# Attention's value products in bursts of nine key blocks, from a ring of twelve

## The chip, the cores and the metric

The kernel runs on one core of a Trainium2 chip. The metric is device time in microseconds (us), as a median over runs. The core's engines have queues of their own and wait for one another through semaphores: TensorE (PE, with PEld for its weight loads), VectorE (DVE), ScalarE (ACT), GpSimd (POOL) and SyncE (SP, which issues most transfers).

## The reference, cut to what matters

Two layers over 2048 latent rows and 256 context rows: multi-head latent attention (16 heads), then gated linear attention. The change lies in the first. Latent queries read all 2304 keys, context queries only the 256 context keys.

```python
def attention_blocks(q, k, v):
    ...
    def one_block(qi):
        s = jnp.einsum('bqhrd,bkhd->bhrqk', qi, k, preferred_element_type=F32) * scale
        p = jax.nn.softmax(s, axis=-1).astype(v.dtype)
        return jnp.einsum('bhrqk,bkhe->bqhre', p, v)
...
def mla_mixer(...):
    oc = attention_blocks(qc, kc, vc)
    ox = attention_blocks(qx, jnp.concatenate([kc, kx], axis=1), jnp.concatenate([vc, vx], axis=1))
    def out(o, gate):
        return (o.reshape(b, n, MLA_WIDTH) * jax.nn.silu(gate)) @ w_out
```

## The kernel before, in words

**The steps.** Attention runs over 8 pairs of heads. Each pair has 5 query chunks, so there are 40 steps: chunk 0 is the 256 context queries (2 key blocks of 128), chunks 1 to 4 are 512 latent queries each (18 key blocks, `kt` 0 to 17). One item is one key block of one step, 592 in all. The order of the work is written out by hand: PE's and most of VectorE's instructions in attention stand in program order (`pe_op`), and the framework places the rest, GpSimd's among them, on in-order queues.

**One item.** First the search for row maxima of a later step is fed one move further (`stream`, L491: 4 matmuls into `pmx`, whose maxima VectorE takes at L493). Then `scores` makes 10 matmuls into `st` (L629), on half the array's rows each, and ScalarE's exponential writes the weights to a slot of `ring` (L631). The ring has 9 slots of 128 x 1024.

**The bursts.** The value products (`values`, L678, full rows and half the columns of the array, fp32 in two passes) come in bursts of six blocks: after `kt` 6 of a step for `kt` 0 to 5, and so on; the last burst of a step comes after item 0 of the next. A context step's two blocks come four items after its second one. With 8 context and 32 x 3 latent bursts, there are 104.

**The sums.** The softmax denominator is the sum of a step's weights over its blocks. VectorE sums the first three blocks of each burst in four instructions (`thirds`, L662), the first time into `acc`, later into `part`. GpSimd adds the other three blocks and `part` to `acc`, one instruction of 128 x 1024 each (`add`, L652). So a latent step has 12 VectorE sums and 11 GpSimd adds: nine blocks and two parts. Blocks that come before the first `thirds` wait in a list.

**The end of a step.** `finish` runs in the burst after a step's last one. It multiplies `acc` with ones on PE (L693, into `pmx`), ScalarE turns that into a reciprocal (L695, L696), and GpSimd scales the output (`ob`, L697). So PE's L693 waits for GpSimd's last add of the step. For chunk 4 of a pair, the next burst is the short one of the next pair's context step, five items after chunk 4's last burst began; for the other chunks it is the next step's first.

**What else GpSimd does.** It splits queries (`qs<-qf`, L48 and L53) and the keys of a later pair (`kbs<-kf`) into high and low parts. Keys go into the buffer that the running pair is reading, piece by piece as chunk 4 has read them for the last time, so five key splits fall around the last chunk of a pair.

**Other parts.** `mods` puts modulation products (L72, L86, L98) behind some bursts. `kbs0` is 8192 columns wide, of which keys use 4608. Near the end of attention `out_weights` splits the output weights into the key buffers, in pieces of 128 x 1024, on ScalarE and GpSimd.

Of the kernel before, what the change touches and what calls it, by code (L numbers as in the profile page):

```python
# [122 lines left out]
def body(ctx, tc, I, out, stop=99, dbg=None):  # L123
# [293 lines left out]

    kbs = [kvp.tile([P, 8 * D], F32R, name="kbs0"), kvp.tile([P, 4 * T], F32R, name="kbs1")]
    kb = [[kbs[b][:, s * T:s * T + T] for s in range(2)] for b in range(2)]
# [183 lines left out]
    with pool("p3", 2) as sp, pool("ps3", 2, space=PSUM) as psp:  # L603
# [5 lines left out]

        RING = 9  # L610
        ring = sp.tile([P, RING, 2, 512], F32, name="pe", bufs=1)

        def scores(si, kt, nk):
            pr, ci = steps[si]
            n = CHUNKS[ci][1]
            kh, kl = kb[pr % 2]
            qs = qss[si]
            if kt == 0:
                assert si in closed
                gt = sp.tile([P, 512], F32, name="gt")  # L620
# [9 lines left out]
            pe = ring[:, slot(si, kt)]  # L630
# [4 lines left out]
        def slot(si, kt):  # L635
            pr, ci = steps[si]
            return (75 * pr + (3 + 18 * (ci - 1) if ci else 0) + kt) % RING

# [15 lines left out]
        def thirds(si, kt):  # L654

            st_ = live[si]
            part = sp.tile([P, 2, 512], F32, name="part", bufs=1) if kt else st_["acc"]
            s0 = slot(si, kt)
            for j in range(2):
                for c in (0, 256):  # L660
                    src = ring[:, s0:s0 + 3, j, c:c + 256].rearrange("p s c -> p c s")
                    pe_op(nc.vector.tensor_reduce(part[:, j, c:c + 256], src, axis=AX.X, op=ALU.add))  # L662
            if kt:
                add(si, part)
            else:
                st_["open"] = True
                for pe in st_["wait"]:
                    add(si, pe)

        def values(si, kt, nk):  # L670
# [3 lines left out]
            if kt == 0:  # L674
                st_["po"] = psp.tile([P, 512], F32, name="po", bufs=1)
            po, pe, vt = st_["po"], ring[:, slot(si, kt)], vts[pr]
            for j in range(2):
# [42 lines left out]
        def first_y(oh, ol):  # L720

            ps = [pmp.tile([P, 512], F32, name="pmx") for _ in range(2)]
            for kt in range(KT):
                for u in range(2):
                    us = slice(u * 512, u * 512 + 512)
                    for i, (a, b) in enumerate(((oh, 0), (oh, 1), (ol, 0))):
                        nc.tensor.matmul(ps[u], a[:, kt, :], wo[kt][b][:, us], start=(kt == i == 0), stop=(kt == KT - 1 and i == 2))
            y0 = ring[:, 0]
# [14 lines left out]
        def out_weights(b, raw):  # L743

            w = kvp.tile([P, 8 * D], F32R, name=f"wo{b}", tag=f"kbs{b}")
            w2 = [w[:, 4 * D * s:4 * D * s + 4 * D].rearrange("p (k n) -> p k n", k=4) for s in range(2)]
            for kt in range(4):
                tc.keep_in_program_order(k.hi("a", w2[0][:, kt, :], raw[kt]))
                tc.keep_in_program_order(k.lo("p", w2[1][:, kt, :], raw[kt], w2[0][:, kt, :]))
                wo[4 * b + kt] = (w2[0][:, kt, :], w2[1][:, kt, :])  # L750

# [3 lines left out]
        rate = (sum(20 if ci else 2 for _, ci in steps) - fed) / (len(items) - 24)  # L755
        fed0 = fed
        pinned = True
        done, extra, nv, nb = [], mods(), 0, 0

        bursts = {i + (4 if nk == 2 else 1): i + 1 for i, (si, kt, nk) in enumerate(items) if kt % 6 == 5 or kt == nk - 1}  # L760

        def burst(i):
# [4 lines left out]
            nb += 1  # L767
            if fed < fed0 + rate * i:
                fed += 1
# [18 lines left out]
            for c in cl:  # L788
                next(c, None)
            if nb > 4 and nb % 3 == 0 and i < len(items) - 70:  # L790
                next(extra, None)

        for i, (si, kt, nk) in enumerate(items):
# [7 lines left out]
            if i % 3 == 1:  # L801
                fetch(1)
            if fed < fed0 + rate * (i + 1):
                fed += 1
# [78 lines left out]
    with pool("p4", 2) as sp, pool("ps4", 2, space=PSUM) as psp:  # L883
# [53 lines left out]
        for t in range(NT):  # L937
# [14 lines left out]
            for u in range(2 if t else 0):  # L952
                us = slice(u * 512, u * 512 + 512)
                p_ = psp.tile([P, 512], F32, name="py", bufs=3)
                k.mm3(p_, [(oh[:, kt, :], ol[:, kt, :], wo[kt][0][:, us], wo[kt][1][:, us]) for kt in range(KT)])
                ps.append(p_)
# [610 lines left out]
```

## Time and profile before

| | us |
|---|---|
| median of 3 runs | 3642.26 |
| lowest, highest | 3637.54, 3643.7 |
| profiled execution | 3641.14 |
| its span, first to last instruction | 3639.3 |
| first and last value product (L678) of attention start | 698.9, 2255.1 |

In the 1556 us of the last row all eight pairs are done. The rows are read so: the timeline merges neighbouring instructions of one kind into one line with their count, and gives in brackets the idle time ahead of it and what ended it; the waits say which engine and line waited for which; the stretches give the busy time of each engine and the clock granted to PE as a share of its full one. A matmul's end is modelled, so starts are compared with starts.

### The profile page before, as it was taken

How to read it: one execution, taken by the hardware profiler on the slowest of the kernel's cores; microseconds unless marked ns; L12 is line 12 of the kernel's file. 1: busy time of each engine (PE TensorE's matmuls, PEld its weight loads, DVE VectorE, ACT ScalarE, POOL GpSimd, SP SyncE). 2: the span in 40 equal slices, each digit the busy share in tenths (PEclk: the TensorE clock that was granted, in tenths of full speed). 3: DMA queues.
4: the chain of work that ended last, by engine and by line, in shares of the span. 5: the costliest groups of instructions: out<-in, count | busy, mean ns of one | idle time of the engine just before them, and what ended most of it. 6: DMA issues, size and time to landing. Idle time of an engine off the chain costs nothing.

```text
span 3639.3 us, 59322 instructions
## 1 busy us (share of the span) xinstructions
PE 3512.7 (97%) x24126; PEld 2657.4 (73%) x24126; DVE 2266.6 (62%) x3350; ACT 1337.6 (37%) x1951; POOL 1418.4 (39%) x873
## 2 busy tenths in 40 slices
PE   6999999999999999999999999999999999999899
PEld 5877887666666666666666665778998998998677
DVE  4333334677777777777777773563277677777753
ACT  2222121244444343444344444232244344454431
POOL 3111205366676666766676677552000001000000
PEclk9999999999999999999999999999999999999899
DMA  6111356402112111202110010777756757678432
GB/s 232 70 67 64 129 219 193 131 24 83 46 36 65 50 53 45 79 18 79 47 58 22 23 40 22 233 234 242 262 197 206 249 173 237 209 235 288 142 118 93
DMA packets 280920, 456.00 MB, mean 125 GB/s; under 512 B 23028, under 2 KB 179764, under 8 KB 268680
## 3 DMA queue, kind: packets, MB, share of 16 engines
q1 hardware_dynamic: 215760, 375.06, 31.2%
q10 hardware_dynamic: 64888, 77.16, 6.2%
q8 instruction: 189, 3.10, 0.3%
q14 instruction: 83, 0.68, 0.1%
HBM read 311.27 MB, written 140.71 MB: 124 GB/s over the span
## 4 chain that ended last, share of the span: by engine, by line
PE 78%; DMA 6%; issue 6%; DVE 5%; POOL 3%; ACT 2%; SPq 1%; ACTq 0%; POOLq 0%; DVEq 0%
PE st L629 18%; PE po L678 14%; PE pmx L491 8%; PE pj L60 5%; PE pj L62 4%; PE pj L61 4%; PE pp L985 3%; PE pp L986 3%; PE pp L987 3%; DMA wsg<-in_gla_w_in 2%; PE py L62 2%; PE py L61 2%; PE py L60 2%; PE pk L1152 1%; PE py L985 1%
## 5 line engine op out<-in xcount | busy, mean ns | idle before, releaser
L493 DVE TENSOR_REDUCE mx<-pmx 128x1 f32<-128x512 f32 (+1 forms) x1312 | 767.4, 627 | 326.6 <-PE pmx L491 316.1
L631 ACT ACTIVATE pe<-st 128x1024 f32<-128x1024 f32 (+1 forms) x592 | 600.8, 1015 | 704.1 <-PE st L629 479.1
L652 POOL TENSOR_TENSOR acc<-acc,pe 128x1024 f32<-128x1024 f32 x288 | 688.2, 2390 | 418.5 <-DVE acc L662 268.3
L629 PE MATMUL st<-qs,kbs 64*128 64x512 f32 (+3 forms) x5920 | 801.9, 390 | 1.5 <-DMA qs<-mr 1.2
L629 PEld LDWEIGHTS st<-qs,kbs 64*128 64x128 f32 (+1 forms) x5920 | 584.2, 185 | 105.1 <-ACT pe L631 4.7
L678 PE MATMUL po<-pe,vt 128*64 128x512 f32 (+1 forms) x2368 | 524.2, 591 | 0.0
L491 PE MATMUL pmx<-kbs,qs 64*128 64x512 f32 (+1 forms) x2624 | 435.4, 380 | 14.2 <-DVE mx L493 13.9
L678 PEld LDWEIGHTS po<-pe,vt 128*64 128x64 f32 x2368 | 160.6, 137 | 310.0 <-issue 306.6
L491 PEld LDWEIGHTS pmx<-kbs,qs 64*128 64x128 f32 x2624 | 271.5, 187 | 127.5 <-issue 43.3
L985 PE MATMUL pp<-w,ht 128*128 128x256 f32 x1088 | 317.3, 292 | 0.0
L986 PE MATMUL pp<-w,ht 128*128 128x256 f32 x1088 | 305.1, 280 | 0.0
L987 PE MATMUL pp<-w,ht 128*128 128x256 f32 x1088 | 304.3, 280 | 0.0
L1334 POOL TENSOR_TENSOR orr<-oss,mhalf 128x4 f32<-128x4 f32 x16 | 17.1, 1069 | 657.4 <-DVE oss L1333 657.4
L662 DVE TENSOR_REDUCE part<-pe 128x256 f32<-128x768 f32 x256 | 246.6, 1027 | 23.5 <-ACT pe L631 19.2
L985 PEld LDWEIGHTS pp<-w,ht 128*128 128x128 f32 x1088 | 204.9, 188 | 3.5
L986 PEld LDWEIGHTS pp<-w,ht 128*128 128x128 f32 x1088 | 205.1, 189 | 1.1
L987 PEld LDWEIGHTS pp<-w,ht 128*128 128x128 f32 x1088 | 204.8, 188 | 0.1
L985 PE MATMUL pp<-ht,w 128*128 128x256 f32 (+1 forms) x616 | 182.9, 297 | 10.8 <-ACT vge L1050 9.1
L119 POOL TENSOR_TENSOR rs_r<-rs_v,mhalf 128x1 f32<-128x1 f32 x52 | 29.3, 564 | 383.5 <-DVE rs_v L117 355.2
L986 PE MATMUL pp<-ht,w 128*128 128x256 f32 (+1 forms) x616 | 175.1, 284 | 0.0
L987 PE MATMUL pp<-ht,w 128*128 128x256 f32 (+1 forms) x616 | 174.3, 283 | 0.1
L1209 ACT ACTIVATE ex<-df 128x512 f32<-128x512 f32 x192 | 114.2, 632 | 145.5 <-DVE df L1206 129.1
(369 smaller groups left out, 6291.6 us busy)
## 6 DMA issues: line engine op xcount, KB each, us to landing
ht<-hh_d SPq DMA_DIRECT2D x44, 1024.0 KB
ht<-hl_d SPq DMA_DIRECT2D x44, 1024.0 KB
xt<-in_x SPq DMA_DIRECT2D x32, 512.0 KB
mod_w<-in_ada_w SPq DMA_DIRECT2D x16, 1024.0 KB
v<-gv_d SPq DMA_DIRECT2D x32, 512.0 KB
wsg<-in_gla_w_in SPq DMA_DIRECT2D x66, 192.0 KB
v_d<-vs ACTq DMA_DIRECT2D x18, 512.0 KB
vt<-v_d SPq DMA_DIRECT2D x8, 1152.0 KB
```

Source lines behind the costliest of these rows:

```text
L60: nc.tensor.matmul(ps, ah, bh, start=(i == 0), stop=False)
L61: nc.tensor.matmul(ps, ah, bl, start=False, stop=False)
L491: pe_op(nc.tensor.matmul(ps[j][:, :w], qs[js, 0, i, t * P:t * P + P], kk[js, bs], start=(i == 0), stop=(i == 1)))
L493: pe_op(nc.vector.reduce_max(mx[:, j * nq + t, b:b + 1], ps[j][:, :w], axis=AX.X))
L629: pe_op(nc.tensor.matmul(st[:, j, :n], a[js, ks], qs[js, s, r, :n], start=(i == 0), stop=(i == len(terms) - 1)))
L631: nc.scalar.activation(pe[:, :, :n], st[:, :, :n], AF.Exp, scale=SCALE)
L652: nc.gpsimd.tensor_tensor(acc, acc, part, op=ALU.add)
L662: pe_op(nc.vector.tensor_reduce(part[:, j, c:c + 256], src, axis=AX.X, op=ALU.add))
L678: pe_op(nc.tensor.matmul(po[64 * j:64 * j + 64, :n], vt[:, kt, 64 * j:64 * j + 64], pe[:, j, :n], start=(kt == 0), stop=(kt == nk - 1)))
L985: nc.tensor.matmul(ps, ah, bh, start=(i == 0), stop=False)
L986: nc.tensor.matmul(ps, ah, bl, start=False, stop=False)
L987: nc.tensor.matmul(ps, al, bh, start=False, stop=(i == n - 1))
```

## The change

The part of `kbs0` that keys leave free becomes a tile of its own, `ring3`, with three more slots: twelve slots in four groups of three, used in turn. Bursts take nine blocks, so a latent step has two; VectorE sums three blocks at `kt` 0 and at `kt` 9 (8 instructions), and GpSimd adds the other twelve blocks and one `part`. From chunk 4 of pair 6 on (`late`), ring and bursts are as before, because part of the output weights goes where `ring3` was. There are 8 + 27 x 2 + 5 x 3 = 77 bursts. The search is fed up to three moves further ahead, and several moves in one burst if it is behind; `mods` moves every second burst instead of every third; the output weights are split in pieces of 128 x 512.

```diff
-    kbs = [kvp.tile([P, 8 * D], F32R, name="kbs0"), kvp.tile([P, 4 * T], F32R, name="kbs1")]
+    kbs = [kvp.tile([P, 2 * T], F32R, name="kbs0"), kvp.tile([P, 4 * T], F32R, name="kbs1")]
+    ring3 = kvp.tile([P, 8 * D - 2 * T], F32, name="ring3")
...
-        RING = 9
-        ring = sp.tile([P, RING, 2, 512], F32, name="pe", bufs=1)
+        ring = sp.tile([P, 9, 2, 512], F32, name="pe", bufs=1)
+        threes = [ring[:, 3 * g:3 * g + 3] for g in range(3)]
+        threes.append(ring3[:, 0:3 * D].rearrange("p (s j c) -> p s j c", s=3, j=2))
+        LAST = 25 * 7 - 6
+        late = lambda si: steps[si][0] == NPAIR - 1 or steps[si] == (NPAIR - 2, len(CHUNKS) - 1)
+        bl = lambda si: 6 if late(si) else 9
+        on_v = lambda si: (0, 6, 12) if late(si) else (0, 9)
...
-            if nk == 2 or kt % 6 > 2:
+            if nk == 2 or kt - kt % 3 not in on_v(si):
                 add(si, pe)
...
+            g = 25 * pr + (1 + 6 * (ci - 1) if ci else 0) + kt // 3
+            return threes[g % 4 if g < LAST else g % 3]
...
-            w = kvp.tile([P, 8 * D], F32R, name=f"wo{b}", tag=f"kbs{b}")
...
+            w = kvp.tile([P, 8 * D if b else 2 * T], F32R, name=f"wo{b}", tag=f"kbs{b}")
+            hs = [w[:, c:c + 512] for c in range(0, (16 if b else 9) * 512, 512)]
+            if b == 0:
+                w = kvp.tile([P, 8 * D - 2 * T], F32R, name="wo2", tag="ring3")
+                hs += [w[:, c:c + 512] for c in range(0, 7 * 512, 512)]
...
+                for u in range(2):
+                    us = slice(u * 512, u * 512 + 512)
+                    h_, l_ = hs[2 * kt + u], hs[8 + 2 * kt + u]
+                    tc.keep_in_program_order(k.hi("a", h_, raw[kt][:, us]))
+                    tc.keep_in_program_order(k.lo("p", l_, raw[kt][:, us], h_))
...
-        bursts = {... if kt % 6 == 5 or kt == nk - 1}
+        bursts = {... if kt % bl(si) == bl(si) - 1 or kt == nk - 1}
...
-            if fed < fed0 + rate * i:
+            while fed < min(fed0 + EARLY * min(1, i / 100) + rate * i, 656):
...
-                if nk > 2 and kt % 6 == 0:
+                if nk > 2 and kt in on_v(si):
                     thirds(si, kt)
...
-            if nb > 4 and nb % 3 == 0 and i < len(items) - 70:
+            if nb > 4 and nb % 2 == 0 and i < len(items) - 70:
```

GpSimd's queue at the end of the last chunk of pair 2, up to the last add into that chunk's `acc` (`kbs` is a key split, `qs` a query split, `pe` and `ring` are slots of the ring). Before:

```order
L652 TENSOR_TENSOR acc<-acc,pe 128x1024 x3
L652 TENSOR_TENSOR acc<-acc,part 128x1024
L48 TENSOR_SCALAR kbs_3830<-kf 128x512
L53 TENSOR_TENSOR kbs_3830<-kf,kbs_3830 128x512
L652 TENSOR_TENSOR acc<-acc,pe 128x1024 x2
L48 TENSOR_SCALAR qs<-qf 128x1024
L53 TENSOR_TENSOR qs<-qf,qs 128x1024
L652 TENSOR_TENSOR acc<-acc,pe 128x1024
L48 TENSOR_SCALAR kbs_3830<-kf 128x512
L53 TENSOR_TENSOR kbs_3830<-kf,kbs_3830 128x512
L652 TENSOR_TENSOR acc<-acc,part 128x1024
```

Ahead of these rows stand the chunk's first three adds, an output product `ob` and a key split: from the first `thirds` on there are 11 adds and three key splits. In the changed kernel, from the fourth add on:

```order
L663 TENSOR_TENSOR acc<-acc,ring_3832 128x1024 x3
L708 TENSOR_TENSOR ob<-ob,rs 128x512
L663 TENSOR_TENSOR acc<-acc,pe 128x1024
L48 TENSOR_SCALAR kbs_3830<-kf 128x512
L53 TENSOR_TENSOR kbs_3830<-kf,kbs_3830 128x512
L663 TENSOR_TENSOR acc<-acc,pe 128x1024 x4
L48 TENSOR_SCALAR qs<-qf 128x1024
L53 TENSOR_TENSOR qs<-qf,qs 128x1024
L663 TENSOR_TENSOR acc<-acc,pe 128x1024
L48 TENSOR_SCALAR kbs_3830<-kf 128x512
L53 TENSOR_TENSOR kbs_3830<-kf,kbs_3830 128x512
L663 TENSOR_TENSOR acc<-acc,part 128x1024
```

Now three adds stand ahead, so there are 13 adds and two key splits; the third key split moved ahead of the chunk's first add. The ends of pairs 0 to 5 have this same order.

PE's queue at the first burst of the last chunk of pair 1 (`st` are scores, `po` value products, `pmx<-acc,ones` the sum of `finish`, `pmx<-ident,mc` a step of the search). Before:

```order
L629 MATMUL st<-qs,kbs_3831 128x512 x10
L678 MATMUL po<-pe,vt 64x512 x12
L693 MATMUL pmx<-acc,ones 64x512 x2
L491 MATMUL pmx<-kbs_3830,qs 128x256 x2
L491 MATMUL pmx<-kbs_3831,qs 128x256 x2
L629 MATMUL st<-qs,kbs_3831 128x512 x10
```

In the changed kernel:

```order
L636 MATMUL st<-qs,kbs_3831 128x512 x10
L492 MATMUL pmx<-kbs_3830,qs 128x512 x2
L492 MATMUL pmx<-kbs_3831,qs 128x512 x2
L689 MATMUL po<-pe,vt 64x512 x18
L704 MATMUL pmx<-acc,ones 64x512 x2
L506 MATMUL pmx<-ident,mc 8x128
L492 MATMUL pmx<-kbs_3830,qs 128x512 x2
```

The burst comes three items later, holds nine blocks instead of six, and takes the search's transposition (L506) with it, which had stood behind the chunk's second burst.

## Rows read from the trace of the kernel before

**Rows 1.** The page: busy us (share of the span) and instructions of two engines.

```profile
PE 3512.7 (97%) x24126; PEld 2657.4 (73%) x24126; DVE 2266.6 (62%) x3350; ACT 1337.6 (37%) x1951; POOL 1418.4 (39%) x873
```

**Rows 2.** Busy us of each engine in attention, 700 to 2260 us; then the granted clock.

```profile
700.00:2260.00 1560.00, 1546.39 (x11071) 973.16 (x11071) 1141.36 (x1755) 656.33 (x688) 1064.52 (x533) 1.00 0.15 47
```

**Rows 3.** Waits of PE in 700 to 2262 us: total, times, longest.

```profile
PE pmx L491 <- DVE mx L493: 8.6, 8, 1.7
PE pmx L693 <- POOL acc L652: 3.1, 1, 3.1
```

**Rows 4.** Timeline of PE around one burst of six: start, length, count.

```profile
1264.19 0.63 PE L491 MATMUL pmx<-kbs,qs 64*128 64x512 f32 x4
1264.75 5.37 PE L678 MATMUL po<-pe,vt 128*64 128x512 f32 x24
1270.05 0.27 PE L505 MATMUL pmx<-ident,mc 128*8 128x128 f32 x1
1270.25 0.73 PE L491 MATMUL pmx<-kbs,qs 64*128 64x512 f32 x4
1270.82 1.33 PE L629 MATMUL st<-qs,kbs 64*128 64x512 f32 x10
1271.98 0.62 PE L491 MATMUL pmx<-kbs,qs 64*128 64x512 f32 x4
1272.44 1.33 PE L629 MATMUL st<-qs,kbs 64*128 64x512 f32 x10
```

**Rows 5.** Timeline of PE's weight loads inside the same burst.

```profile
1265.23 0.14 PEld L678 LDWEIGHTS po<-pe,vt 128*64 128x64 f32 x2 [0.29 <-issue]
...
1269.09 0.14 PEld L678 LDWEIGHTS po<-pe,vt 128*64 128x64 f32 x2 [0.29 <-issue]
```

**Rows 6.** Timeline of POOL, chunk 4 of pair 2 from its first add.

```profile
1253.70 7.32 POOL L652 TENSOR_TENSOR acc<-acc,pe 128x1024 f32<-128x1024 f32 x3 [5.71 <-DVE acc L662]
1260.99 1.30 POOL L697 TENSOR_TENSOR ob<-ob,rs 128x512 f32<-128x512 f32 x1
1262.24 0.63 POOL L48 TENSOR_SCALAR kbs<-kf 128x512 fp32r<-128x512 f32 x1
...
1264.21 7.26 POOL L652 TENSOR_TENSOR acc<-acc,pe 128x1024 f32<-128x1024 f32 x3
...
1281.36 1.04 POOL L48 TENSOR_SCALAR qs<-qf 128x1024 fp32r<-128x1024 f32 x1
...
1284.80 2.38 POOL L652 TENSOR_TENSOR acc<-acc,pe 128x1024 f32<-128x1024 f32 x1
...
1289.56 2.40 POOL L652 TENSOR_TENSOR acc<-acc,part 128x1024 f32<-128x1024 f32 x1
```

**Rows 7.** Timeline of PE there: first burst of the chunk, and its sum.

```profile
1248.62 5.37 PE L678 MATMUL po<-pe,vt 128*64 128x512 f32 x24
...
1295.05 1.03 PE L693 MATMUL pmx<-acc,ones 128*64 128x512 f32 x4
```

**Rows 8.** Timelines of PE and POOL in chunk 4 of pair 1: first burst, last add, sum.

```profile
1047.70 2.79 PE L678 MATMUL po<-pe,vt 128*64 128x512 f32 x12
...
1088.59 2.40 POOL L652 TENSOR_TENSOR acc<-acc,part 128x1024 f32<-128x1024 f32 x1
...
1093.62 1.03 PE L693 MATMUL pmx<-acc,ones 128*64 128x512 f32 x4
```

**Rows 9.** Timeline of PE at a modulation product.

```profile
1232.88 1.92 PE L72 MATMUL pmx<-mod_w,condT 128*32 128x512 f32 x16
...
1238.52 0.72 PE L491 MATMUL pmx<-kbs,qs 64*128 64x512 f32 x3 [1.65 <-DVE mx L493]
```

**Rows 10.** Stretches after two of PE's waits: busy us by engine, then granted clock.

```profile
1240.50:1244.00 3.50, 3.50 (x26) 3.01 (x26) 1.12 (x3) 1.58 (x2) 0.00 (x0) 0.69 0.97 366
2259.80:2263.30 3.50, 3.50 (x10) 2.76 (x9) 0.55 (x2) 1.23 (x2) 3.50 (x2) 0.51 0.00 0
```

**Rows 11.** Timeline of POOL at the end of attention.

```profile
2258.77 9.40 POOL L53 TENSOR_TENSOR wo<-wso,wo 128x1024 fp32r<-128x1024 f32 x4
```

More of the change, by code (lines that the diff above doesn't have):

```diff
@@ L629, in scores, with three, weights @@
                     pe_op(nc.tensor.matmul(st[:, j, :n], a[js, ks], qs[js, s, r, :n], start=(i == 0), stop=(i == len(terms) - 1)))
-            pe = ring[:, slot(si, kt)]
+            pe = weights(si, kt)
             nc.scalar.activation(pe[:, :, :n], st[:, :, :n], AF.Exp, scale=SCALE)
-            if nk == 2 or kt % 6 > 2:
+            if nk == 2 or kt - kt % 3 not in on_v(si):
                 add(si, pe)
-        def slot(si, kt):
+        def three(si, kt):
             pr, ci = steps[si]
-            return (75 * pr + (3 + 18 * (ci - 1) if ci else 0) + kt) % RING
+            g = 25 * pr + (1 + 6 * (ci - 1) if ci else 0) + kt // 3
+            return threes[g % 4 if g < LAST else g % 3]
+        def weights(si, kt):
+            return three(si, kt)[:, kt % 3]
         def add(si, part):
@@ L657, in thirds @@
             part = sp.tile([P, 2, 512], F32, name="part", bufs=1) if kt else st_["acc"]
-            s0 = slot(si, kt)
+            t3 = three(si, kt)
             for j in range(2):
                 for c in (0, 256):
-                    src = ring[:, s0:s0 + 3, j, c:c + 256].rearrange("p s c -> p c s")
+                    src = t3[:, :, j, c:c + 256].rearrange("p s c -> p c s")
                     pe_op(nc.vector.tensor_reduce(part[:, j, c:c + 256], src, axis=AX.X, op=ALU.add))
@@ L675, in values @@
                 st_["po"] = psp.tile([P, 512], F32, name="po", bufs=1)
-            po, pe, vt = st_["po"], ring[:, slot(si, kt)], vts[pr]
+            po, pe, vt = st_["po"], weights(si, kt), vts[pr]
             for j in range(2):
@@ L726, in first_y @@
                     for i, (a, b) in enumerate(((oh, 0), (oh, 1), (ol, 0))):
-                        nc.tensor.matmul(ps[u], a[:, kt, :], wo[kt][b][:, us], start=(kt == i == 0), stop=(kt == KT - 1 and i == 2))
+                        nc.tensor.matmul(ps[u], a[:, kt, :], wo[kt][b][u], start=(kt == i == 0), stop=(kt == KT - 1 and i == 2))
             y0 = ring[:, 0]
@@ L743, in out_weights @@
         def out_weights(b, raw):
-            w = kvp.tile([P, 8 * D], F32R, name=f"wo{b}", tag=f"kbs{b}")
-            w2 = [w[:, 4 * D * s:4 * D * s + 4 * D].rearrange("p (k n) -> p k n", k=4) for s in range(2)]
-            for kt in range(4):
-                tc.keep_in_program_order(k.hi("a", w2[0][:, kt, :], raw[kt]))
-                tc.keep_in_program_order(k.lo("p", w2[1][:, kt, :], raw[kt], w2[0][:, kt, :]))
-                wo[4 * b + kt] = (w2[0][:, kt, :], w2[1][:, kt, :])
+            w = kvp.tile([P, 8 * D if b else 2 * T], F32R, name=f"wo{b}", tag=f"kbs{b}")
[3 more added lines that the diff above has]
+                hs += [w[:, c:c + 512] for c in range(0, 7 * 512, 512)]
+            for kt in range(4):
+                wo[4 * b + kt] = (hs[2 * kt:2 * kt + 2], hs[8 + 2 * kt:10 + 2 * kt])
+                for u in range(2):
[3 more added lines that the diff above has]
+                    tc.keep_in_program_order(k.lo("p", l_, raw[kt][:, us], h_))
         items = [(si, kt, (CTX if ci == 0 else T) // P) for si, (pr, ci) in enumerate(steps) for kt in range((CTX if ci == 0 else T) // P)]
@@ L756, in body @@
         fed0 = fed
+        EARLY = 3
         pinned = True
         done, extra, nv, nb = [], mods(), 0, 0
-        bursts = {i + (4 if nk == 2 else 1): i + 1 for i, (si, kt, nk) in enumerate(items) if kt % 6 == 5 or kt == nk - 1}
+        bursts = {i + (4 if nk == 2 else 1): i + 1 for i, (si, kt, nk) in enumerate(items) if kt % bl(si) == bl(si) - 1 or kt == nk - 1}
         def burst(i):
@@ L802, in body @@
                 fetch(1)
[L803 removed]
+            if fed < fed0 + EARLY * min(1, i / 100) + rate * (i + 1):
                 fed += 1
@@ L954, in body @@
                 p_ = psp.tile([P, 512], F32, name="py", bufs=3)
-                k.mm3(p_, [(oh[:, kt, :], ol[:, kt, :], wo[kt][0][:, us], wo[kt][1][:, us]) for kt in range(KT)])
+                k.mm3(p_, [(oh[:, kt, :], ol[:, kt, :], wo[kt][0][u], wo[kt][1][u]) for kt in range(KT)])
                 ps.append(p_)
```

## The prediction, made before the changed kernel was run

> **What bounds the kernel now.** I read the page first, then the stretch of attention, then the waits of PE in it, and last the timelines of PE and GpSimd at the two places that the change touches: a burst, and the end of a pair. The page shows PE busy for 97% of the span and GpSimd for 39% [rows 1]. In attention PE is busy for 1546 of 1560 us, GpSimd for 1065 and VectorE for 1141 [rows 2], so PE bounds this stage. It waits little: 8.6 us in 8 places for VectorE's maxima, and 3.1 us once, at the very end, for GpSimd's last add [rows 3]. There are thus two ways in which this change can move the time: fewer PE cycles, or new waits on PE.
>
> The reader should also see a near miss. At the end of pair 2, GpSimd's last add ends at 1289.56 + 2.40 = 1291.96, and PE's sum of it starts at 1295.05 [rows 6, 7]: a slack of 3.1 us. At the end of pair 1 it is 1093.62 - 1090.99 = 2.6 us [rows 8]. GpSimd is busy for two thirds of the stage, but right there it is nearly late.
>
> **Fewer bursts: a gain.** A burst changes how PE's array is used (half the rows for scores, half the columns for values). From the search to values it takes 1264.75 - 1264.19 = 0.56 us, from the search to scores 0.46: 0.10 more [rows 4]. The first pair of value matmuls lasts 1265.23 - 1264.75 = 0.48 us, a pair further on (1269.09 - 1265.23) / 9 = 0.43: 0.05 more. The last pair starts at 1269.52 and what follows at 1270.05: 0.10 more. The search behind the burst takes 0.57 instead of 0.46: 0.11 more [rows 4, 5]. That is 0.36 us for a burst on the path. With 104 - 77 = 27 fewer: 9.7 us gained. The bounds are 5.4 (entry and exit alone) and 9.7; I take 9.7, since all four pieces stand in the rows.
>
> The Trainium skill says in "TensorEngine Tiling (Array Packing)", Key Properties, that a change of tiling mode drains the engine, and in "TensorE: Matmul & The Clock Gate", Step-by-step: what each phase is for, that a drain is about 128 cycles. At the full clock that would be an estimate of 0.05 us each way and of 2.9 us for 27 bursts, and the sum below would end 6.8 us higher. The rows show over three times as much, and they decide.
>
> **Later and more adds on GpSimd: the loss.** At the end of a pair the sum of `finish` comes five items after the start of chunk 4's last burst, not a whole burst later as elsewhere. I compare two paths from the same point, the start of that chunk's first burst.
>
> GpSimd's path in the changed kernel: in pair 2 the first add starts 1253.70 - 1248.62 = 5.1 us after the burst, when VectorE has its three blocks. Behind it stand, without a gap, 13 adds at 2.43 us (7.32 and 7.26 for three: 31.6), one `ob` at 1.25, two key splits at 1.97 (3.9) and one query split at 1284.80 - 1281.36 = 3.44 [rows 6, 7]. The end is at 5.1 + 31.6 + 1.25 + 3.9 + 3.4 = 45.3 us. The weights that the adds read are there in time. The chunk before has the same chain without key splits, 41.4 us, and a chunk takes about 1556 / 32 = 48.6 us with its share of context steps, so GpSimd has some 7 us for the first three key splits and is free when the burst comes.
>
> PE's path: in pair 1, without a modulation on the way, it is 1093.62 - 1047.70 = 45.9 us [rows 8]. The new first burst comes three items later (3 x 1.62 = 4.9, from 1.16 + 0.46 of [rows 4]), and one burst boundary falls away (0.4). Both hold 18 blocks of values, the context's two and the same sums. That leaves 40.6 us, so PE waits for 45.3 - 40.6 = 4.7 us. The order shows this queue at the ends of pairs 0 to 5; pair 6 keeps bursts of six there. At the ends of pairs 0, 2 and 4, one modulation product lies on PE's path in the new order: 1.9 us, and a wait behind it of 1.65 less the usual 0.2 [rows 9]. There PE waits for 4.7 - 3.3 = 1.4 us. Waits: 3 x 4.7 + 3 x 1.4 = 18.3 us. Bounds: 9 (PE 1.7 us later than that throughout) and 30 (2 us sooner).
>
> After such a wait PE's clock falls. After the wait of 3.1 us in [rows 3], the granted clock is 0.51 over 3.5 us; behind the wait of 1.65 us it is 0.69 over 3.5 [rows 10]. The first costs 1.7 us of work at the full clock. I take 1.7 for each long wait and half of that for each short one: 5.1 + 2.6 = 7.7 us, with bounds of 5.1 (the long ones alone) and 15 (twice as long).
>
> The Trainium skill speaks against moving sums to GpSimd: "GPSIMD Engine Reference", Elementwise side-by-side cycle accounting and Engine selection, wants an elementwise add on VectorE and gives 4.5 us for an add of twice this size. By an estimate of 2.25 us for one, the chain would end 2.3 us sooner, the waits would be 7.2 us and the sum 11 us lower. The rows have 2.43 from start to start and decide.
>
> **What else moves.** The four VectorE instructions less per step (27 x 4) free an engine for which PE waits 8 times in all [rows 3], and the one looked at stands behind a modulation [rows 9], of which there are as many as before. I take 0; the bound is a gain of those 8.6 us. The search does the same number of moves, a few items earlier, and in the new order its results are ready eight items ahead of their use instead of five: 0. The key and query splits end 2 to 3 us later in their chunk; the first search that reads such a query stands some five items behind the pair's sum, about 8 us: 0. The ring is no tighter: a slot is written again twelve items later instead of nine, and by the chain above GpSimd's adds have left it by then. Halving the pieces of the output weights puts eight instructions in the place of four at the end, where they hold up the last output: four take 9.40 us [rows 11]; eight of half the size, at 1.3 as the lower key split in [rows 6] has (1.97 less 0.63), 10.4. A cost of 0.9 us; the same halving earlier lies beside PE's scores.
>
> **The sum.** -9.7 + 18.3 + 7.7 + 0.9 = +17.2 us on the profiled execution's 3641.1, so 3658.3. The median of the runs is 1.1 us above that execution: 3659.4. I forecast 3659 us, 0.5% slower. About 0.2%, or 7.3 us, is what a measurement here can tell from no change.
>
> **The rivals.**
> - GpSimd is not late, and only the gain is left: 3642.3 - 9.7 + 0.9 = 3633.5, faster. It needs the chain of 45.3 us to end 4.7 us sooner, which is the price of the two added adds (4.9), or PE to come as much later. For it speaks that GpSimd idles for a third of the stage. Against it: that idle time lies ahead of the chain, where it waits for VectorE's three blocks (5.7 us ahead of the first add [rows 6]), and inside the chain hardly any is left to close. Chance 8%.
> - PE comes later than I count, so the waits shrink to about 9 us and the clock falls at half the places: 3642.3 - 9.7 + 9 + 3.9 + 0.9 = 3646.4, no change that can be told. Its own waits behind the longer bursts would do that. Chance 18%.
> - The waits are as long as the upper bounds, and the clock stays low twice as long: 3642.3 - 9.7 + 30 + 15 + 0.9 = 3678.5. A key split that must wait for its transfer inside the chain would do that. Chance 9%.
> - The change doesn't do what it says: the 0.36 us are no cost of a burst but of what comes with it, such as the sums and transpositions, whose number stays. Then there is no gain, and the waits are left: 3669, inside the forecast's range. Chance 5%.
>
> **How the numbers follow.** The forecast has 60%, with a range of its own from 3648 to 3670. The range for 8 in 10 leaves out the first rival and most of the third: 3642 to 3676. Faster by over 0.2%: the first rival, 8%. Within 0.2%: the second and a little of the forecast's lower end, 19%. Slower: 73%.
>
> **What the profile after would show.** Right: PE's waits have a row of L704 (the sum, L693 before) for GpSimd's add with six more places, long ones at the ends of pairs 1, 3 and 5, each with a dip of the clock behind it; and entries and exits of bursts as long as before, only 27 fewer. Wrong: no such waits (then the first rival), or GpSimd's last add in those chunks ending less than 43 us after the chunk's first burst, or more than 47.

## The result, and the profile after

| | before | changed |
|---|---|---|
| median of 4 runs each, us | 3642.98 | 3693.80 |
| lowest, highest | 3637.54, 3643.83 | 3689.76, 3694.28 |
| ratio, 95% interval | | 1.0135 [1.0123, 1.0148] |
| span of the profiled execution | 3639.3 | 3691.7 |
| attention, first to last value product | 698.9 to 2255.1 (1556.3) | 698.2 to 2308.4 (1610.3) |

The changed kernel is 1.35% slower (51 us by the medians), where 17 us were forecast. The sign was right, the time lies outside the range. All of the loss lies in attention: +54.0 us there, and what follows the last value product takes 1384 us before and 1383 after.

The page of the changed kernel, the row that answers [rows 1]:

```profile
PE 3525.7 (96%) x24126; PEld 2693.1 (73%) x24126; DVE 2167.9 (59%) x3242; ACT 1338.6 (36%) x1959; POOL 1547.9 (42%) x935
```

VectorE has 108 instructions less and GpSimd 62 more, as planned. Now attention by engine, then granted clock, DMA share and GB/s (answers [rows 2]):

```profile
700.00:2310.00 1610.00, 1559.22 (x11060) 1007.63 (x11056) 1042.76 (x1646) 657.13 (x695) 1191.28 (x590) 0.98 0.15 46
```

PE was busy for 1546 of 1560 us before; now it idles for 51 of 1610, and the mean clock has gone from 1.00 to 0.98. What PE waits for in that stretch (total, times, longest; answers [rows 3]):

```profile
PE pmx L704 <- POOL acc L663: 14.4, 4, 5.3
PE st L636 <- DMA qs<-mr: 14.0, 2, 8.5
PE pmx L492 <- DVE mx L494: 13.1, 10, 2.2
PE pmx L492 <- ACT mod_g L100: 6.5, 2, 3.4
PE pmx L492 <- DVE mr L510: 1.3, 5, 0.3
```

Of these the kernel before had only the maxima (8.6) and one short wait for the transfer of the maxima row:

```profile
PE st L629 <- DMA qs<-mr: 1.2, 1, 1.2
```

So three kinds of wait are new: for GpSimd's sum (forecast), for the transfer that puts the row of maxima into the queries (`qs<-mr`), and for ScalarE's copy of a modulation gate (`mod_g`). With 0.2 us more on either side, waits rose from 10.0 to 49.5 us: +39.5, of which 14.4 are the sum's, 12.8 the transfer's, 6.5 the gate copies', and the rest the maxima's and their row's. The trace's clock records add up to 6.8 us at the lower of the clock's two levels (half speed) in attention before, 58.0 after. Part of that lies inside the waits: PE was busy in 44.9 of the 58.0 us, and in all of the 6.8 before. 38.1 us more of work at half speed cost some 19 us. 39.5 + 19 = 58.5 us lost, against 54 measured: 4 to 5 us are left for the gain.

**The wait that was forecast.** PE and then GpSimd at the end of pair 1 (answers [rows 8]):

```profile
1072.63 7.95 PE L689 MATMUL po<-pe,vt 128*64 128x512 f32 x36
...
1112.18 1.08 PE L689 MATMUL po<-pe,vt 128*64 128x256 f32 x8
1118.62 1.98 PE L704 MATMUL pmx<-acc,ones 128*64 128x512 f32 x4 [5.35 <-POOL acc L663]
```

```profile
1078.01 14.70 POOL L663 TENSOR_TENSOR acc<-acc,pe 128x1024 f32<-128x1024 f32 x6 [4.40 <-DVE acc L673]
...
1114.30 0.62 POOL L48 TENSOR_SCALAR kbs<-kf 128x512 fp32r<-128x512 f32 x1 [0.51 <-DMA kf<-k_d]
1115.00 1.26 POOL L53 TENSOR_TENSOR kbs<-kf,kbs 128x512 fp32r<-128x512 f32 x1
1116.22 2.34 POOL L663 TENSOR_TENSOR acc<-acc,part 128x1024 f32<-128x1024 f32 x1
```

GpSimd's last add ends 1116.22 + 2.34 - 1072.63 = 45.9 us after the chunk's first burst (forecast: 45.3). PE is done with its own work 1112.18 + 1.08 - 1072.63 = 40.6 us after it (forecast: 40.6).

**The wait that was not.** The end of pair 4, on PE, ScalarE's queue, SP's queue and GpSimd:

```profile
1727.55 0.79 PE L636 MATMUL st<-qs,kbs 33*128 33x512 f32 x1 [5.55 <-DMA qs<-mr]
```

```profile
1719.78 6.68 ACTq L512 DMA_DIRECT2D qs<-mr  x2
```

```profile
1710.61 1.81 SPq L453 DMA_DIRECT2D qf<-qr_d  x4
1723.35 0.34 SPq L436 DMA_DIRECT2D kf<-k_d  x1
1727.93 0.34 SPq L450 DMA_DIRECT2D qf<-qn_d  x1
```

```profile
1720.97 2.36 POOL L53 TENSOR_TENSOR qs<-qf,qs 128x1024 fp32r<-128x1024 f32 x1
1723.28 2.34 POOL L663 TENSOR_TENSOR acc<-acc,pe 128x1024 f32<-128x1024 f32 x1
1725.93 0.62 POOL L48 TENSOR_SCALAR kbs<-kf 128x512 fp32r<-128x512 f32 x1 [0.31 <-DMA kf<-k_d]
...
1727.86 2.37 POOL L663 TENSOR_TENSOR acc<-acc,part 128x1024 f32<-128x1024 f32 x1
```

Read from the last fence up: GpSimd's query split ends at 1723.3 and frees a buffer; SP can then issue the key load (1723.35), and its data are there at 1725.9. Only then does ScalarE's queue issue the second of the two small transfers: the two take 6.68 us to issue, until 1726.46. PE starts again at 1727.55. The transfer of the maxima has nothing to do with that key load by its data. What ties them is a completion semaphore: the program gives every transfer one of a few, which the transfer raises when it has landed, and the next transfer with the same one waits for that before it is issued. In the program's instructions the key load on SP and the second of ScalarE's two transfers share `DMAHW6`, one right after the other:

```
L436 DMA kf<-k_d 128x512 [waits DMAHW6_49,Pool_49]
L512 DMA qs<-mr 1x4x128 [waits DMAHW5_49,DMAHW0_49,DVE_49]
L512 DMA qs<-mr 1x4x128 [waits DMAHW6_49]
```

The end of pair 5 is the same, with 9.59 us on ScalarE's queue and 8.49 us on PE. At these two ends the late sum cannot be seen: GpSimd's last add ends at 1730.2, before PE, now itself held up by 5.55 us, comes to its sum.

**The gate copy.** The end of pair 0, on PE, ScalarE and SP's queue:

```profile
907.97 1.22 PE L492 MATMUL pmx<-kbs,qs 64*128 64x512 f32 x4 [3.10 <-ACT mod_g L100]
```

```profile
907.33 0.59 ACT L100 COPY mod_g<-pmx 128x512 f32<-128x512 f32 x1 [7.14 <-DMA gbc_d<-mod_g]
```

```profile
896.93 2.53 SPq L628 DMA_DIRECT2D gt<-gate_d  x1
900.17 0.33 SPq L450 DMA_DIRECT2D qf<-qn_d  x1
900.55 1.81 SPq L453 DMA_DIRECT2D qf<-qr_d  x4
902.41 0.43 SPq L628 DMA_DIRECT2D gt<-gate_d  x1
903.15 0.34 SPq L101 DMA_DIRECT2D gbc_d<-mod_g  x1
```

One buffer serves both gate copies of a modulation block. The first copy's store stands on SP's queue behind the loads of the next pair and leaves at 903.15; the second copy waits 7.14 us for it. PE's search waits for that copy, which reads the `pmx` buffer that the search needs next. Modulation now goes on in every second burst instead of every third, and this put a gate right behind the sum at the end of pair 0. The other wait, of 3.40 us at 1058 us, lies inside pair 1: there the first store stands behind a key load that SP issued at 1053.73, when GpSimd's query split had ended.

**The clock.** Stretches behind four of the waits (answers [rows 10]; the granted clock is the third number from the end):

```profile
896.00:900.00 4.00, 3.69 (x7) 1.38 (x8) 0.00 (x0) 1.63 (x3) 2.00 (x3) 0.64 0.63 178
...
1115.00:1122.00 7.00, 3.38 (x12) 1.48 (x14) 0.22 (x1) 1.23 (x2) 5.38 (x4) 0.54 0.41 115
...
1726.00:1733.00 7.00, 5.45 (x26) 4.26 (x28) 2.49 (x4) 2.65 (x3) 5.20 (x5) 0.54 0.29 78
1931.00:1942.00 11.00, 5.00 (x26) 3.97 (x28) 2.04 (x4) 2.65 (x3) 8.78 (x6) 0.53 0.24 64
```

With a wait of 2.1 us the clock was at its lower level for 3.4 us, with 5.4 and 5.6 us for 6.8, with 8.5 us for 10.2; with the gate copies' 3.1 and 3.4 us it was 6.8. In the long waits it fell before PE had started again, which is why the second stretch has PE idle and the clock low at once. The forecast had 3.5 us for each long wait.

**The bursts.** One of nine blocks, PE and its weight loads (answers [rows 4, 5]):

```profile
1301.43 7.95 PE L689 MATMUL po<-pe,vt 128*64 128x512 f32 x36
1309.31 0.73 PE L492 MATMUL pmx<-kbs,qs 64*128 64x512 f32 x4
1309.88 0.75 PE L636 MATMUL st<-qs,kbs 64*128 64x256 f32 x10
```

```profile
1301.92 0.14 PEld L689 LDWEIGHTS po<-pe,vt 128*64 128x64 f32 x2 [0.29 <-issue]
...
1308.35 0.14 PEld L689 LDWEIGHTS po<-pe,vt 128*64 128x64 f32 x2 [0.28 <-issue]
```

The first pair takes 0.49 us, a pair further on 0.43, the search behind it 0.57: these pieces of an entry and an exit cost what they cost before.

### The profile page after: what moved, and what is told of

Same layout as the page of the kernel before. It is cut to its first block, busy times and chain, and to the rows that moved or that the text cites. A ratio compares the mean times of both kernels' runs of the same rounds, so it can differ in the third digit from the quotient of the medians.

```text
span 3691.7 us, 59328 instructions
## 1 busy us (share of the span) xinstructions
PE 3525.7 (96%) x24126; PEld 2693.1 (73%) x24126; DVE 2167.9 (59%) x3242; ACT 1338.6 (36%) x1959; POOL 1547.9 (42%) x935
## 4 chain that ended last, share of the span: by engine, by line
PE 70%; DMA 8%; POOL 8%; issue 6%; DVE 5%; ACT 2%; SPq 1%; ACTq 0%; POOLq 0%; DVEq 0%
PE st L636 16%; PE po L689 11%; PE pmx L492 7%; PE pj L60 4%; PE pj L61 4%; PE pj L62 4%; POOL acc L663 4%; PE pp L1004 3%; PE pp L1006 3%; PE pp L1005 3%; DMA wsg<-in_gla_w_in 2%; PE py L1004 1%; PE py L62 1%; PE py L61 1%; PE py L60 1%
## 5 line engine op out<-in xcount | busy, mean ns | idle before, releaser
L636 PE MATMUL st<-qs,kbs 64*128 64x512 f32 (+2 forms) x5920 | 839.5, 394 | 14.3 <-DMA qs<-mr 14.0
L636 PEld LDWEIGHTS st<-qs,kbs 64*128 64x128 f32 (+1 forms) x5920 | 628.7, 188 | 110.3 <-DMA qs<-mr 14.7
L638 ACT ACTIVATE pe<-st 128x1024 f32<-128x1024 f32 (+1 forms) x467 | 473.3, 1014 | 507.8 <-PE st L636 401.5
L492 PE MATMUL pmx<-kbs,qs 64*128 64x512 f32 (+1 forms) x2624 | 475.8, 383 | 25.9 <-DVE mx L494 18.0
L689 PE MATMUL po<-pe,vt 128*64 128x512 f32 (+1 forms) x1868 | 413.3, 589 | 0.0
L492 PEld LDWEIGHTS pmx<-kbs,qs 64*128 64x128 f32 x2624 | 309.6, 190 | 123.6 <-issue 39.9
L689 PEld LDWEIGHTS po<-pe,vt 128*64 128x64 f32 x1868 | 128.6, 137 | 247.8 <-issue 243.8
L1353 POOL TENSOR_TENSOR orr<-oss,mhalf 128x4 f32<-128x4 f32 x16 | 17.1, 1069 | 657.7 <-DVE oss L1352 657.7
L663 POOL TENSOR_TENSOR acc<-acc,ring 128x1024 f32<-128x1024 f32 x81 | 194.6, 2403 | 79.6 <-DVE acc L673 75.0
L638 ACT ACTIVATE ring<-st 128x1024 f32<-128x1024 f32 (+1 forms) x125 | 127.5, 1021 | 132.3 <-PE st L636 124.1
```

The source lines that it names most:

```text
L492: pe_op(nc.tensor.matmul(ps[j][:, :w], qs[js, 0, i, t * P:t * P + P], kk[js, bs], start=(i == 0), stop=(i == 1)))
L663: nc.gpsimd.tensor_tensor(acc, acc, part, op=ALU.add)
L689: pe_op(nc.tensor.matmul(po[64 * j:64 * j + 64, :n], vt[:, kt, 64 * j:64 * j + 64], pe[:, j, :n], start=(kt == 0), stop=(kt == nk - 1)))
```

## The experiments

Each is told by its ratio to the kernel before, timed beside it on the same chip; differences in us are those of the medians. The medians of before were 3637.19 (e1 to e4), 3641.52 (e5 to e8), 3634.72 (e9, e10), 3638.94 (e11, e12) and 3642.20 (e13, e14).

### Which part of the change makes the sum late

**e1_last_six**: the last chunk of every pair keeps bursts of six and three sums.

```diff
+        six = lambda si: late(si) or steps[si][1] == len(CHUNKS) - 1
-        bl = lambda si: 6 if late(si) else 9
-        on_v = lambda si: (0, 6, 12) if late(si) else (0, 9)
+        bl = lambda si: 6 if six(si) else 9
+        on_v = lambda si: (0, 6, 12) if six(si) else (0, 9)
```

> The changed kernel, but the last query chunk of every pair keeps bursts of six with three VectorE sums and 11 GpSimd adds; the chunks 1 to 3 keep bursts of nine and 13 adds, so there are 83 bursts. Theory (GpSimd's queue is late at a pair's end, and all else follows from that): no wait of the sum at a pair's end over 1 us, no wait of the scores for the maxima's transfer over 2 us, about 3643 - 21 x 0.36 + 1 = 3636 us (3630 to 3644). Rival (the burst of nine itself, the earlier search or the faster modulations cost the time): three of four latent chunks still have it, so about 3680 us (3672 to 3690).

**e2_three_sums**: bursts of nine, but three sums a step on VectorE.

```diff
-        on_v = lambda si: (0, 6, 12) if late(si) else (0, 9)
+        on_v = lambda si: (0, 6, 12)
```

> The changed kernel with VectorE's sums as before (at key blocks 0, 6 and 12), so 11 GpSimd adds a step; bursts of nine and the ring of twelve stay. Theory: GpSimd's chain at a pair's end is 4.9 us shorter, 40.4 against 40.6 us on PE's path, so the waits there fall to 0 to 1 us each and the time to about 3640 us (3634 to 3650). Rival (the bursts): unchanged, 3685 to 3696 us.

**e3_later_sum**: the last denominators of a pair three items later.

```diff
-            while done:
+            hold = group[-1][2] == 2 and group[-1][0] > 0 and not late(done[-1] if done else 0)
+            while done and not hold:
                 finish(done.pop(0))
...
+            if steps[si][1] == 1 and kt == 6 and len(done) > 1:
+                finish(done.pop(0))
```

> The changed kernel, but the sum of a pair's last step is made three items later, behind item 6 of the next pair's first latent chunk instead of in the context step's burst; GpSimd's queue is not shortened. Theory: the five waits of that sum (17.5 us in the changed kernel) go, with the low clock behind them (about 8 us), but the waits for transfers that stand behind GpSimd's lateness (14 us for the maxima, 6.5 us for the modulation's store) stay: 3665 to 3677 us. Rival (the lateness acts on PE through that sum alone): all goes, 3632 to 3645 us. Rival (the bursts): 3685 to 3696 us.

**e4_two_sums_six**: the kernel before (bursts of six, ring of nine) with VectorE's sums only at `kt` 0 and 12.

```diff
-            if nk == 2 or kt % 6 > 2:
+            if nk == 2 or kt - kt % 3 not in (0, 12):
...
-                if nk > 2 and kt % 6 == 0:
+                if nk > 2 and kt in (0, 12):
```

> The kernel before with one thing of the change: VectorE sums at key blocks 0 and 12 alone, so GpSimd has 13 adds a step; ring of nine and bursts of six stay. Theory: the slack of 2.6 to 3.1 us at a pair's end turns into waits of about 2 us at seven places, with some low clock and the transfers behind them: 3658 to 3685 us. Rival (the bursts): 3638 to 3648 us, as before.

Measured: e1 3650.67, ratio 1.0035 [1.0023, 1.0046]; e2 3652.06, 1.0039 [1.0026, 1.0051]; e3 3668.17, 1.0080 [1.0061, 1.0098]; e4 3654.18, 1.0045 [1.0031, 1.0060]. The waits for the sum, of e2 and of e3 (each with the 3.1 us at the very end of attention, which the kernel before has too):

```profile
PE pmx L704 <- POOL acc L663: 3.9, 3, 3.1
```

```profile
PE pmx L704 <- POOL acc L663: 3.3, 2, 3.1
```

Each of the three ways to give GpSimd less, or PE more time, takes away the waits for the sum, and between 20 and 37 us of the 51. So that theory holds as far as it goes. e3 came where it was expected. But e1 and e2 should have been near the kernel before or below it, and are 13 and 15 us above it, outside their ranges: something else costs. Their traces say what. In e2 it is spread out: 4.2 us of waits for the transfer, 2.7 for a gate copy, 12.0 for maxima, and 17.1 us at the lower clock. In e1 it is the gate copy alone, in three places:

```profile
PE pmx L492 <- ACT mod_g L100: 15.5, 3, 8.4
```

In e4, two sums without the longer bursts cost 17 us. The waits for the sum are short there (1.7 us); PE waits 5.5 us for the transfer of the maxima, 12.5 for maxima, and 17.1 us are at the lower clock. The expectation had the direction and too high a price (its range began at 3658).

### The waits nobody forecast

**e5_gates_apart**: the changed kernel, its second gate copy one step of `mods` later.

```diff
         for j in range(gates):
+            if j and bufs == 1:
+                yield
             pt = bank()
```

> The changed kernel, with the two gate copies of a modulation block one step (two bursts) apart, so that the second copy does not stand and wait for the store of the first. Theory: in the changed kernel TensorE waited 3.3 and 3.6 us at these copies (6.5 us) and 6.8 us of low clock followed each, of which half is lost (6.8): both go, 3694 - 13 = 3681 us (3676 to 3687). Rival: TensorE only catches up with work that would have waited at the next pair end anyway: 3690 to 3695.

**e6_search_early**: the changed kernel, its search led by six pieces instead of three.

```diff
-        EARLY = 3
+        EARLY = 6
```

> The changed kernel, with the search for the maxima led by six pieces in place of three, so that by the order each result stands at least eight row blocks ahead of its use (two, at the ends of pairs 4 and 5, in the changed kernel). Theory: the waits for the maxima's transfer (5.8 and 8.8 us, with 6.8 and 10.2 us of low clock behind them) go, 23 us; behind them the late GpSimd sums of these two ends come out, as at the four ends before: about 2.1 and 5 us, with 3.4 and 6.8 us of low clock, 12 us. 3694 - 11 = 3683 us (3676 to 3688), and six waits for the sum in place of four. Rival A: the transfer is late for another reason than its small lead, and the waits stay: 3691 to 3695. Rival B: the sums are not late there: 3671.

**e9_two_more_dma**: the changed kernel with four transfers of 32 bytes more.

```diff
         pe_op(nc.vector.reduce_max(mc[:, :2 * nq], mx[:, :2 * nq, :npart], axis=AX.X))
+        if si in (26, 31):
+            for r in range(2):
+                pe_op(nc.scalar.dma_start(tiny_d[r], mc[0:1, 0:2 * nq]))
```

> The changed kernel, with two transfers of 32 bytes more on ScalarE's queue, at the ends of pairs 4 and 5 alone, issued when the maxima are ready, some 7 us before the two transfers of the maxima row. Nothing else differs. Theory: the transfers of a program take a fixed few completion semaphores in turn, and one cannot be issued until the one before it on the same semaphore has landed; the second transfer of the maxima row has that of the key load that waits for its buffer. Two more in the order move the row's transfers on to the semaphores of the two small ones, which have long landed: the waits of 5.8 and 8.8 us go, the late sums (2 and 5 us) come out as in e6_search_early, and a program with more transfers runs about 9 us faster: 3685 us (3680 to 3690). Rival: ScalarE's queue is late because of the key load's traffic or of the search itself: more transfers help nothing, 3693 to 3697.

Measured: e5 3678.49, 1.0089 [1.0068, 1.0111]; e6 3685.29, 1.0123 [1.0106, 1.0140]; e9 3680.18, 1.0126 [1.0107, 1.0145].

e5: the waits for `mod_g` are gone, and 14 us with them (13 expected, from waits of 3.3 and 3.6 us; by the trace's rows they were 3.1 and 3.4). At the end of pair 5 another ScalarE copy, of a modulation block (`mod_s`), has come to stand behind the blocked queue, and its row on ScalarE names the cause outright:

```profile
1911.69 9.57 ACTq L514 DMA_DIRECT2D qs<-mr  x2
1921.30 0.58 ACT L78 COPY mod_s<-pmx 128x512 f32<-128x512 f32 x1 [18.63 <-DMA kf<-k_d]
```

e6: the waits for the transfer are gone and the sum waits in six places instead of four, besides the one at the very end, as expected:

```profile
PE pmx L704 <- POOL acc L663: 23.9, 7, 5.2
```

e9 tells why the transfer was late. The two small ones move those of the maxima on to other semaphores, and nothing else is changed. ScalarE's queue, SP's queue and PE at the end of pair 4:

```profile
1717.09 1.24 ACTq L516 DMA_DIRECT2D qs<-mr  x2
```

```profile
1720.70 0.34 SPq L437 DMA_DIRECT2D kf<-k_d  x1
```

```profile
1727.70 1.76 PE L708 MATMUL pmx<-acc,ones 128*64 128x512 f32 x4 [1.68 <-POOL acc L667]
```

The two transfers are issued in 1.24 us instead of 6.68, 2.4 us ahead of the key load and not behind its landing, at the same lead of the search as in the changed kernel. So it was the shared semaphore, and neither the search's lead as such nor the load's traffic; a longer lead only hides it. In time e6 and e9 are 7 and 5 us nearer to the kernel before than the changed kernel (4 and 3 by the ratios), where 11 and 9 were expected; the intervals overlap with the changed kernel's, so the traces carry this verdict and not the times. Their attention lasts 1602.3 and 1605.2 us, against 1610.3. One reason can be read: in e9 the clock is low for as long as in the changed kernel (58.0 us), among it 10.2 us after a wait of 2 us.

### All of it taken away, and a faster kernel

**e7_six_gates**: e1_last_six with the gate copies apart.

```diff
+            if j and bufs == 1:
+                yield
```

> Bursts of six with three sums in the last chunk of every pair (as in the run e1_last_six), and the two gate copies of a modulation block a step apart. Theory: what held e1_last_six above the kernel before was the gate copies alone, 15.5 us of waits and half of some 14 us of low clock: 3651 - 22 = 3629 us (3624 to 3634), below the kernel before, since the longer bursts do save what was counted. Rival: the bursts of nine save nothing on this path: 3636 to 3645.

**e8_later_early_gates**: e3_later_sum with the gate copies apart and the longer lead.

```diff
+            if j and bufs == 1:
+                yield
...
-        EARLY = 3
+        EARLY = 6
```

> The changed kernel with all three waits taken away at once, bursts of nine and two sums kept: the pair's last denominators three row blocks later (as in e3_later_sum), the search led by six pieces, the gate copies a step apart. Theory: the three waits and the low clock behind them are all that the change lost: e3_later_sum's 3668 - 13.8 - 10.1 - half of some 30 us of low clock = 3629 us (3623 to 3638). Rival: two sums instead of three load GpSimd so that something else is late in their place: 3645 or more.

**e10_three_early_gates**: e2_three_sums with the same two edits as e8.

> Bursts of nine in every chunk as in the changed kernel, but three sums on VectorE (as in e2_three_sums), the search led by six pieces and the gate copies a step apart. It differs from e8_later_early_gates (3641 us) by the three sums, with the pair's last sum at its old place. Theory A, two sums cost nothing but the lateness at the pair ends: 3641 us (3637 to 3645). Theory B, the two sums cost some 5 to 10 us more, spread out, by GpSimd's six added adds for each pair that lie on what TensorE's search waits for: 3630 us (3626 to 3635), since 27 bursts less save more than the 21 of e7_six_gates (3631).

**e12_three_six_gates**: e7_six_gates with three sums everywhere.

```diff
-        on_v = lambda si: (0, 6, 12) if six(si) else (0, 9)
+        on_v = lambda si: (0, 6, 12)
```

> e7_six_gates with three sums on VectorE in every chunk, bursts kept (nine, six in the last chunk of a pair). Theory: two sums cost nothing where the pair's end is not behind them: ratio to the kernel before 0.997 to 0.998, as for e7_six_gates. Rival: GpSimd's added adds cost a few us spread out: ratio 0.9955 to 0.9965.

**e11_all_six**: e12_three_six_gates with bursts of six everywhere.

```diff
-        bl = lambda si: 6 if six(si) else 9
+        bl = lambda si: 6
```

> e7_six_gates with bursts of six and three sums everywhere, everything else of the change kept (twelve slots, halves of the output weights, pace of the modulation and of the search). It differs from e7_six_gates by 21 bursts more and by the two sums. Theory: the gain of e7_six_gates below the kernel before (10 us) is the bursts', 21 at 0.23 to 0.36 us: 5 to 8 us come back, and the time lies 2 to 5 us below that of the kernel before, ratio 0.9985 to 0.9995. Rival: the bursts are worth nothing and the gain came with the paces and the gate copies: ratio 0.997 to 0.998.

| run | median, us | ratio to before, 95% interval | low clock in attention, us | attention, us | PE's work in it, us |
|---|---|---|---|---|---|
| kernel before | 3642.98 | 1 | 6.8 | 1556.3 | 1542.4 |
| changed kernel | 3693.80 | 1.0135 [1.0123, 1.0148] | 58.0 | 1610.3 | 1538.0 |
| e7_six_gates | 3631.47 | 0.9974 [0.9965, 0.9983] | 0.0 | 1548.6 | 1536.4 |
| e8_later_early_gates | 3641.41 | 1.0000 [0.9991, 1.0009] | 0.0 | 1553.7 | 1540.0 |
| e10_three_early_gates | 3639.57 | 1.0008 [0.9998, 1.0017] | 3.4 | 1555.0 | 1538.0 |
| e11_all_six | 3636.31 | 0.9993 [0.9985, 1.0002] | 3.4 | 1552.6 | 1543.2 |
| e12_three_six_gates | 3629.70 | 0.9976 [0.9967, 0.9986] | 3.4 | 1550.8 | 1536.5 |

The last two columns are from one trace of each run: from the first value product to the last, and PE's busy time in that stretch less half of what it did at the lower clock, so waits and clock are out of it (matmul ends are modelled). What follows attention took anything from 1374 to 1386 us in the traces of this study, so a trace is compared by its attention alone.

Attention of e7, by engine and with its clock, and its two largest waits in it (the second stands at the end of attention before, too):

```profile
700.00:2248.00 1548.00, 1535.73 (x11070) 981.26 (x11066) 1061.65 (x1670) 657.02 (x696) 1161.97 (x577) 1.00 0.15 48
```

```profile
PE pmx L494 <- DVE mx L496: 10.5, 11, 2.5
PE pmx L707 <- POOL acc L666: 3.1, 1, 3.1
```

Without the three waits and the low clock behind them the change is a gain, as far as it goes: e7 and e12 are 9 to 10 us faster than the kernel before, the only two of this study that are faster than both kernels by more than 0.2%. Between e11 and e12 only the bursts differ (and with their number the pace of modulation), and 21 fewer are worth 0.9993 - 0.9976 = 0.0017, or 6 us, 0.3 us each; the intervals of the two allow some 2 to 11 us. Their traces split this up: PE's work is 1543.2 - 1536.5 = 6.7 us less, 0.32 us a burst, but attention is only 1.8 us shorter, because PE waits more for the search. PE's waits for maxima, of e11 and of e12:

```profile
PE pmx L494 <- DVE mx L496: 7.0, 6, 1.7
```

```profile
PE pmx L494 <- DVE mx L496: 10.4, 11, 2.5
```

The two sums in nine-block chunks gain nothing (e7 against e12).

e8 missed, and e10 came where its theory A had it, so the two sums are not what e8 lost: with bursts of nine everywhere and hardly a wait left, both are only level with the kernel before. They share two things that e7 and e12 don't have, and two more runs take these apart. **e13_six_early** is e12 with a longer lead:

```diff
-        EARLY = 3
+        EARLY = 6
```

> e12_three_six_gates (9 us below the kernel before) with the search led by six pieces in place of three. In e10_three_early_gates two things differ from e12_three_six_gates: bursts of nine in the last chunk of a pair too, and this lead, and it lies 14 us higher against the kernel before. Theory A, the early search is what costs (VectorE and TensorE do more of it ahead, and run out of it at the end): ratio 1.000 to 1.002. Theory B, the bursts of nine at the pair's end cost: ratio 0.997 to 0.998, unchanged.

**e14_nine_four** is e10 with a shorter one:

```diff
-        EARLY = 6
+        EARLY = 4
```

> e10_three_early_gates with the search led by four pieces in place of six, the least lead at which every result stands six row blocks ahead in the order. Theory A, the early search is what costs: a third of the lead over three remains, so ratio 0.997 to 0.999. Theory B, the bursts of nine at the pair's end cost: ratio about 1.001 as for e10_three_early_gates.

Measured: e13 3636.95, 0.9987 [0.9977, 0.9996]; e14 3634.38, 0.9982 [0.9973, 0.9991]. e14 lies where theory A has it: with the shorter lead, bursts of nine at a pair's end do not undo the gain. e13 lies between the two, 4 us above e12 with overlapping intervals. In the traces a lead of six goes with more work of PE and not with more waits: 1540.0 us in e13 against 1536.5 in e12, 1538.0 in e10 against 1536.7 in e14, and 1540.9 in e6 against the changed kernel's 1538.0. That is 1 to 4 us, so the long lead is part of what e8 and e10 lost. It is not shown to be all: attention lasts 1555.0 us in e10 and 1554.6 in e14, while by their ratios 9 us lie between these two, which were timed on different chips. How the lead adds work to PE, and where the rest went, stays open.

## Why the prediction was right or wrong

- **The bursts, -9.7.** The price held within the error: 0.3 us each by the times of e11 and e12, 0.32 by PE's work in their traces, where 0.36 was read from one burst. In the changed kernel PE's work is 4.4 us less than before, not 9.7, and the six bursts fewer of the pairs' last chunks show no gain at all (1536.7 us in e14 against 1536.5 in e12). The estimate after the Trainium skill's page "TensorE: Matmul & The Clock Gate", Step-by-step: what each phase is for, is lower (2.9 us for 27, or 0.1 us each). The two traces have three times that, but the interval of the two runs' times does not shut it out.
- **The late sum, 18.3.** Held: 14.4 in the four places where it can be seen. The two paths came within 0.6 us of their forecast lengths; PE waited 2.1, 5.4, 2.2 and 4.8 us at the ends of pairs 0 to 3 where 1.4 and 4.7 were forecast in turn, and with the last two ends uncovered (e6, e9) the row has 20.8 and 20.2 us behind the 3.1 of the end. Comparing the two chains from one starting point was the right tool. Six of GpSimd's adds take 14.70 us in the row above, 2.45 each: the duration from the trace before held for the added ones.
- **The clock, 7.7.** Mis-sized: some 19. Two errors add up. The price was taken from a wait of 3.1 us, while the long ones were 5 us and had 6.8 us of low clock behind them, not 3.5; and waits came at places that the sum didn't have. e7, with no low clock, shows what it is to be rid of it.
- **"its results are ready eight items ahead of their use instead of five: 0"**, and **"The key and query splits end 2 to 3 us later in their chunk; [...] 0".** This is the step that failed. The first was read at one pair. The search's last steps are taken only in bursts, so a result that just misses one comes a whole burst later: at the ends of pairs 4 and 5 the order has it ready just two items ahead, in the very place where GpSimd is late (the kernel before had two such places as well, at the ends of pairs 5 and 6, and paid 1.2 us). And the later splits were followed to the search that reads the query, not to the load that waits for its buffer: that load holds SP's queue and, by a shared semaphore, ScalarE's. It cost 14.0 us of waits and 17 us of low clock, in 10.4 of which PE was busy: some 19 us, less the 9 us that the prediction has for the two sums hidden there.
- **The gate copies** had no term. The diff changes the pace of modulation, and the prediction counted its products but not where its stores would stand on SP's queue: 6.5 us of waits and 13.6 us of low clock; e5 gives 14 us back.
- **VectorE's maxima, 0 with a bound of -8.6.** Wrong side: from 8.6 to 13.1 us, 10 waits instead of 8. Freeing VectorE did not help, and longer bursts alone raise these waits: from 7.0 us in e11 to 10.4 in e12, with the same sums in both.
- **The output weights, +0.9.** By its own terms 10.4 less 9.40 is 1.0. It came out as 0.6: at the end of attention the row of [rows 11] is now

```profile
2312.05 9.97 POOL L53 TENSOR_TENSOR wo<-wso,wo 128x512 fp32r<-128x512 f32 x8
```

The third rival (3678.5) named a key split that waits for its transfer inside the chain, and that is there (0.51 us in pair 1's rows), but it was not what cost. The range ended at 3676 because no rival had a new wait that costs time beside the sum's: what else moved had been read at one place each and put at 0.

## What to carry to other kernels

Where an engine that frees buffers becomes later, follow every load that waits for these buffers, and everything queued behind that load or sharing a completion semaphore with it, at each place where it happens and not at one of them. A saving on the busiest engine is worth its full size only if no new wait comes with it: here a wait cost its own length and half of the work that PE then did at the lower clock. When a change is slower than its gain says, put the waits right one at a time; here the late sums of two pairs were hidden behind the transfers (e6, e9).

## What the runs showed of the hardware

- A transfer's issue can be held by another one on another queue, with no data in common, when the program gives both the same completion semaphore: 6.68 and 9.59 us on ScalarE's queue for two transfers, 1.24 and 1.22 us with two small transfers put in ahead (e9). With these four transfers more attention was 5.1 us shorter; the times of the two kernels cannot be told apart.
- The clock's dip grows with the wait, but not strictly: 3.4 us with a wait of 2.1 us, 6.8 with 3.1 to 5.6, 10.2 with 8.5 in the changed kernel; 3.4 with 3.1 us at the end of attention in the kernel before; in e9 10.2 us with a wait of 2 us, and in e6 none at all with 1.7 and 1.9 us.
- Waits cost more than their own length: in e1 15.5 us of gate waits, with 20.5 us of low clock in all, stand between a kernel 13 us slower than before and one 10 us faster (e7).
